# Weight sums of the second feed-forward made early, in the mixer, and kept in DRAM

## The chip, the cores and the metric

The kernel runs on one core of one Trainium2 chip. The core has five engines that run side by side, each with its own in-order list of instructions: TensorE (PE, with its weight loads shown apart as PEld), VectorE (DVE), ScalarE (ACT), GpSimd (POOL) and SyncE (SP). SP and POOL also issue the DMA transfers, which 16 DMA engines carry out. Working memory on the core is SBUF, matmul results go to PSUM, and the inputs lie in DRAM. The metric is the device time of one execution in microseconds; lower is better. The kernel before takes 2007.45 us, the median of 3 runs (2005.02 to 2007.62).

## The reference

One block of a language model on 256 tokens of width 2048, all in float32: a gated feed-forward, a mixer, a second gated feed-forward, each between two normalizations and added to its input.

```python
D_MODEL = 2048; SEQ = 256; D_FF = 5632
def _swiglu(x, w_gate, w_up, w_down):
    return (jax.nn.silu(x @ w_gate) * (x @ w_up)) @ w_down

f = _swiglu(_rmsnorm(h, ln_ffn1_pre), ffn1_gate, ffn1_up, ffn1_down)
h = h + 0.5 * _rmsnorm(f, ln_ffn1_post)
mx = _hybrid_mixer(_rmsnorm(h, ln_mix_pre), w_in, ...)   # RWKV recurrence, pooling, gates, w_out
h = h + _rmsnorm(mx, ln_mix_post)
f = _swiglu(_rmsnorm(h, ln_ffn2_pre), ffn2_gate, ffn2_up, ffn2_down)
h = h + 0.5 * _rmsnorm(f, ln_ffn2_post)
```

The mixer multiplies the tokens by a wide matrix w_in, runs a recurrence over the tokens on one part (16 heads of 64, done in 4 chunks of 64 tokens per half of the heads), sliding averages on another, and joins both through gates and w_out.

## The kernel before, in words

**Products.** The tokens are the stationary side of a matmul (128 rows of the inner dimension by 128 tokens), the weights stream through, 512 columns at a time. For accuracy each float32 operand is split into a high half (a cast to a shorter float format, on ScalarE) and a low half (operand minus high half, on VectorE), and a product is three matmuls: high by high, high by low, low by high (`mm3`, L330, lines L332 to L334). So every weight tile costs one load on SP (`get_w`, L294, into one of 4 buffers `w32`), one cast on ScalarE and one subtraction on VectorE into one of 5 buffers `wH`/`wL` (the "ring"), and then its matmuls. L308/L309 do this in the mixer, L386/L396 for pairs and L639/L644 for quads in the feed-forwards.

**Feed-forward (`ffn`, L1080).** The gate and up matrices are worked through in 11 blocks of 512 columns, two column groups at a time (f and l), then the down matrix in four groups of 512. Block 0 of the gate comes from `gemm_tok`; in the first feed-forward it goes through `head` (L794), a hand-written order for the cold start, in a list of its own. The other blocks come from `seven` (L527), which reads a string of letters. `f` and `l` are a pair: two 128-row tiles of one column group, times both token halves, 12 matmuls. `q` and `Q` are a quad: two row tiles of both column groups at once by the Strassen-Winograd scheme, 7 products instead of 8, so 21 matmuls instead of the 24 of an `f` and an `l`. For it sums of the weights are needed. With a = (f of k, l of k+1) and b = (l of k, f of k+1) they are

```python
t13 = a + (b[0], b[0])        # L622, 1024 columns
t2  = a[0] + t13[1]           # L627, 512 columns
t4  = b[1] + t2               # L631, 512 columns
```

All three are VectorE additions in a `q`. In a `Q` the first is made by a DMA instead: SP loads f of k and l of k+1 (L613), and POOL issues a transfer that adds l of k onto both (L617). In both, four casts (L639) and four subtractions (L644) follow: a (1024 columns), b (512), t13 (1024), t2 with t4 (1024). The corresponding sums of the tokens (`sums`, L435) are made once per stage and shared by the blocks.

**Order of the work.** In the feed-forwards the strings fix TensorE's order. Everything else is put in order by a planner (`Plan.solve`, L143): every operation has an engine, a duration, what it depends on, what buffers it takes, and a due time worked back from TensorE's order. It fills in the earliest operation on each engine, with the transfers' times estimated, and the result is written out as fixed lists for all five engines (`run`, L279). A load is issued at most 22 us ahead of its due time (`FETCH`). General buffers ("units") are 33 tiles of 128 x 1024 float32.

**Mixer (`mixer`).** Only TensorE's order is fixed there: generators yield pieces of matmuls, and the recurrence (`rwkv`, L1977 to L2028 for the scan over chunks) is woven with other products, so that between two of its steps stand 1.6 to 2.8 us of other matmuls, and 44 us ahead of the scan. The other engines' instructions are ordered when the program is compiled, by rank: an instruction's place in the program, or a place that is moved by `high_priority(offset=...)`; the one of lowest rank goes first among those that are ready in the compiler's own timing. The order is then fixed as a list for each engine. `tok_g` (L840) is the product of all tokens with 512 columns, and it is used for w_in and the two projections. `across` (L1047) uses it and then turns the result by a VectorE transpose and 16 small POOL transfers (L1071). The units are held by the tokens (8), the recurrence's registers (15, `R`) and what goes in and out of it. Sums and weights of the feed-forwards are not touched in the mixer.

## Time and profile before

The profile is of one execution on the chip.

| | before |
|---|---|
| median of 3 runs | 2007.45 us |
| profiled execution, its own time | 2005.37 us |
| its span, first to last instruction | 2003.7 us |
| TensorE busy | 1990.0 us, 9903 matmuls |
| VectorE busy | 1813.6 us |
| ScalarE busy | 1224.3 us |
| GpSimd busy | 410.0 us |
| moved by DMA | 472.36 MB, mean 236 GB/s |
| granted TensorE clock | 0.999 of full speed |

The first feed-forward runs from 0 to about 690 us, the mixer to about 1300, the second feed-forward to the end. How to read it: matmuls overlap each other, so the mean of one (about 390 ns) is longer than the step from one start to the next; the number of matmuls in a stretch is the better measure of TensorE's pace. Some matmul records are missing in places. A row "x <- y: total, times, longest" of the list of waits says how long the engine stood still before instruction x until y was done.

### The profile page before, as it was taken

What the parts mean: (1) busy time and instruction counts of PE and PEld (TensorE: products, weight loads), DVE (VectorE), ACT (ScalarE), POOL (GpSimd) and SP (SyncE); (2) the same over time, 40 slices, a digit from 0 to 9 for tenths busy, and PEclk for the clock granted to TensorE, in tenths of its full rate; (3) what the DMA queues carried; (4) which work ended last, traced back from release to release, by engine and by line L of the source; (5) the groups of instructions that cost most, each with busy time, mean ns of one, the idle gap of its engine ahead of it and who ended that gap; (6) DMA issues with size and microseconds to landing.
All of it is one profiled execution on the core that took longest, in us unless ns stands there. A gap on an engine that the chain in (4) does not pass through costs nothing.

```text
span 2003.7 us, 29050 instructions
## 1 busy us (share of the span) xinstructions
PE 1990.0 (99%) x9903; PEld 1644.7 (82%) x9903; DVE 1813.6 (91%) x2462; ACT 1224.3 (61%) x1631; POOL 410.0 (20%) x747
## 2 busy tenths in 40 slices
PE   9999999999999999999999999999999999999998
PEld 7888888888888888888788788888888888888886
DVE  6999999999999957799689678989999999999997
ACT  7566665676665566685466434575666656666563
POOL 2222231323000113412320111012222313230000
PEclk9999999999999999999999999999999999999999
DMA  9788798878778767757556547768888988876784
GB/s 341 226 268 270 216 304 271 254 238 257 211 229 272 264 191 210 206 174 219 147 168 189 169 158 262 263 226 276 265 269 254 276 259 244 258 242 207 232 284 158
DMA packets 253941, 472.36 MB, mean 236 GB/s; under 512 B 27363, under 2 KB 30816, under 8 KB 253792
## 3 DMA queue, kind: packets, MB, share of 16 engines
q1 hardware_dynamic: 213984, 400.89, 60.4%
q0 software_dynamic: 39520, 69.08, 15.3%
q8 instruction: 78, 1.28, 0.3%
q10 hardware_dynamic: 288, 0.52, 0.1%
q14 instruction: 71, 0.58, 0.1%
HBM read 445.45 MB, written 8.39 MB: 227 GB/s over the span
## 4 chain that ended last, share of the span: by engine, by line
PE 93%; DVE 3%; DMA 2%; issue 1%; ACT 0%; SPq 0%; DVEq 0%; POOLq 0%; POOL 0%; ACTq 0%
PE mm L332 25%; PE mm L334 24%; PE mm L333 24%; PE ms L333 5%; PE ms L334 5%; PE ms L332 5%; DMA w<-in_ffn_down_dram 1%; DVE wL L644 1%; PE tr L939 1%; DVE wL L396 1%; DMA w<-in_w_out_dram 0%; PE pA L1881 0%; DVE t L622 0%; PE mc L901 0%; DVE t L627 0%
## 5 line engine op out<-in xcount | busy, mean ns | idle before, releaser
L332 PE MATMUL mm<-wH,xH 128*128 128x512 f32 (+1 forms) x2008 | 784.3, 391 | 2.0 <-ACT wH L386 1.5
L334 PE MATMUL mm<-wH,xL 128*128 128x512 f32 (+1 forms) x2008 | 779.4, 388 | 0.1
L333 PE MATMUL mm<-wL,xH 128*128 128x512 f32 (+1 forms) x2008 | 779.3, 388 | 0.1
L332 PEld LDWEIGHTS mm<-wH,xH 128*128 128x128 f32 x2008 | 377.2, 188 | 80.9 <-ACT wH L386 1.9
L334 PEld LDWEIGHTS mm<-wH,xL 128*128 128x128 f32 x2008 | 377.0, 188 | 78.7 <-DVE xL L957 1.1
L333 PEld LDWEIGHTS mm<-wL,xH 128*128 128x128 f32 x2008 | 377.3, 188 | 75.7 <-DVE wL L309 0.4
L639 ACT CAST wH<-t 128x1024 fp32r<-128x1024 f32 x244 | 257.1, 1055 | 221.2 <-PE mm L334 121.0
L386 ACT CAST wH<-w 128x1024 fp32r<-128x1024 f32 x293 | 302.8, 1053 | 128.6 <-PE mm L334 100.8
L396 DVE TENSOR_TENSOR wL<-w,wH 128x1024 fp32r<-128x1024 f32 x293 | 351.9, 1227 | 13.8 <-ACT wH L386 12.5
L644 DVE TENSOR_TENSOR wL<-t,wH 128x1024 fp32r<-128x1024 f32 x244 | 295.7, 1234 | 10.9 <-ACT wH L639 10.2
L309 DVE TENSOR_TENSOR wL<-w,wH 128x1024 fp32r<-128x1024 f32 (+2 forms) x184 | 217.5, 1190 | 84.6 <-ACT wH L308 83.2
L308 ACT CAST wH<-w 128x1024 fp32r<-128x1024 f32 (+2 forms) x184 | 188.8, 1030 | 167.0 <-PE mm L334 147.5
L639 ACT CAST wH<-w 128x1024 fp32r<-128x1024 f32 x244 | 200.1, 837 | 109.7 <-PE mm L334 75.1
L982 POOL DMA_DIRECT2D x<-T x352 | 180.6, 608 | 389.6 <-DVE T L965 76.1
L644 DVE TENSOR_TENSOR wL<-w,wH 128x1024 fp32r<-128x1024 f32 x244 | 231.6, 966 | 0.9 <-ACT wH L639 0.9
L333 PE MATMUL ms<-wL,sH 128*128 128x512 f32 x312 | 121.5, 389 | 0.2 <-DVE wL L644 0.2
L332 PE MATMUL ms<-wH,sH 128*128 128x512 f32 x312 | 121.4, 389 | 0.0
L334 PE MATMUL ms<-wH,sL 128*128 128x512 f32 x312 | 121.4, 389 | 0.0
L617 POOL DMA_DIRECT2D t<-in_ffn_up_dram x48 | 59.8, 1256 | 230.8 <-DMA t<-in_ffn_up_dram 56.1
L631 DVE TENSOR_TENSOR t<-w,t 128x512 f32<-128x512 f32 x122 | 85.5, 701 | 0.5 <-DMA w<-in_ffn_down_dram 0.2
L627 DVE TENSOR_TENSOR t<-w,t 128x512 f32<-128x512 f32 x122 | 85.3, 700 | 0.3 <-DMA w<-in_ffn_down_dram 0.3
L622 DVE TENSOR_TENSOR t<-w,w 128x1024 f32<-128x1024 f32 x60 | 73.8, 1231 | 2.8 <-DMA w<-in_ffn_down_dram 2.8
(353 smaller groups left out, 2312.4 us busy)
## 6 DMA issues: line engine op xcount, KB each, us to landing
w<-in_w_in_dram SPq DMA_DIRECT2D x128, 512.0 KB, 4.3
w<-in_ffn_down_dram SPq DMA_DIRECT2D x104, 512.0 KB, 6.5
w<-in_ffn_up_dram SPq DMA_DIRECT2D x94, 512.0 KB, 6.0
w<-in_ffn_gate_dram SPq DMA_DIRECT2D x92, 512.0 KB, 6.6
w<-in_ffn_gate_dram SPq DMA_DIRECT2D x168, 256.0 KB, 5.5
w<-in_ffn_down_dram SPq DMA_DIRECT2D x130, 256.0 KB, 4.9
w<-in_ffn_up_dram SPq DMA_DIRECT2D x116, 256.0 KB, 5.9
t<-in_ffn_up_dram POOLq DMA_DIRECT2D x48, 512.0 KB, 8.4
```

The source lines that it names most:

```text
L308: s.nc.scalar.copy(vH, v)
L309: s.nc.vector.tensor_tensor(out=vL, in0=v, in1=vH.bitcast(F32), op=ALU.subtract)
L332: nc.tensor.matmul(ps, aH, bH, start=start, stop=False, skip_group_check=seeded)
L333: nc.tensor.matmul(ps, aH, bL, start=False, stop=False, skip_group_check=seeded)
L334: nc.tensor.matmul(ps, aL, bH, start=False, stop=stop, skip_group_check=seeded)
L386: nc.scalar.copy(x["H"], x["v"])
L396: nc.vector.tensor_tensor(out=x["L"], in0=x["v"], in1=x["H"].bitcast(F32), op=ALU.subtract)
L627: V.tensor_tensor(out=v["t24"][:, 0], in0=v["a"][:, 0], in1=v["t13"][:, 1], op=ALU.add)
L631: V.tensor_tensor(out=v["t24"][:, 1], in0=v["b"][:, 1], in1=v["t24"][:, 0], op=ALU.add)
L639: nc.scalar.copy(H, src)
L644: V.tensor_tensor(out=L, in0=src, in1=H.bitcast(F32), op=ALU.subtract)
L982: nc.gpsimd.dma_start(out=x[0][q * 32:q * 32 + 32, i], in_=src[i * 32:i * 32 + 32, q])
```

## The change

1. **Sums made ahead.** A new generator `premakes` makes, for each quad marked with the new letter `P`, the three sums t13, t2 and t4 of a weight block of the second feed-forward, and writes them to DRAM: four loads of 256 KB on SP, three additions on VectorE, two writes of 512 KB on POOL, with three units held meanwhile. `tok_g` asks for one such set after its row tiles 4, 8 and 12, in the first part of the mixer and again while and after the second half of the recurrence is woven in (`PRE_AT`), not during the first half. All of a set's instructions rank 1500 places later than where they stand (`PRE`).
2. **Second feed-forward.** It gets orders of its own (`GATE_UP2`, `DOWN2`). A `P` quad loads its sums from DRAM (two loads of 512 KB) besides three tiles of 256 KB, and makes no addition. The new orders hold 66 quads (26 q, 17 Q, 23 P), where the old hold 59 (28 q, 31 Q).
3. **First feed-forward.** It keeps 59 quads in a new order (29 q, 30 Q). The planner now takes VectorE as busy for its first 5.5 us there and ScalarE for 4.5 (`TAKEN`), and an operation that may choose a unit instead of its own kind of buffer leaves free those units that operations due earlier need (`kept_for`).
4. **Head in one list.** The list that `head` opens stays open, and the planner's order of the first feed-forward is written behind it in the same list, where before it was a second list.

```diff
-GATE_UP = ["", "fffflQlfqfllll",
-           "fqqflQQQfll", "flflQfqqQfll", ...
+    "fqfqlQQQfll", "flflqqfqQfll", ...
+GATE_UP2 = ["", "fPllfPfPqfll",
+    "flffPqPlfqll", "fqqPllqPffl", "fPfqPlPqlfl",
+    "fqfqPQflPll", "fflqQQPQfll", "fPqPllQPffl",
+    "fqfqlQQfPll", "flPPflqPqfl", "fPlqQPPlffl"]
+DOWN2 = ((0, "ffffffQfffflQqflllfqQlqlllQllQlfflll", 0),
+    (2, "fqffqQflqflQflqqqfffflQfQf", TRAIL))
+TAKEN = dict(DVE=5.5, ACT=4.5)
+PRE = 1500
+PRE_AT = ((4, 8, 12), (), (4, 8, 12))
...
+        def kept_for(n):
+            c = 0
+            for m in takers:
+                if m.due >= n.due or c > NUNITS:
+                    break
+                c += m.units
+            return c
...
-                    u, i = free[k.res[1]], HOLD if r == "ring" else SPARE
+                    u = free[k.res[1]]
+                    i = max(aside + (r == "ring"), HOLD if r == "ring" else SPARE)
...
+            def bring(i):
+                v[("t13", "t24")[i]] = s.unit((P, 2, 512), F32, ("t13", "t24")[i])
+                nc.sync.dma_start(out=v[("t13", "t24")[i]], in_=made(q)[:, i])
+            if ready_made:
+                n13, n4 = [p.op("SP", 0.4, lambda i=i: bring(i), take=[(k13, k24)[i]], size=0.52,
+                                ahead=FETCH) for i in range(2)]
...
         E = mybir.EngineType
-        with s.tc.manual_schedule(engines={E.PE, E.Activation, E.DVE, E.SP}):
+        stack = ExitStack()
+        stack.enter_context(s.listed())
+        with stack:
...
+            s.open = stack.pop_all()
...
+            if k0 in s.pre_at:
+                with s.tc.high_priority(offset=-PRE):
+                    next(s.jobs, None)
...
+    def premakes(s, wg, wu):
+        nc = s.nc
+        for b, order in enumerate(GATE_UP2):
+            quads = [c for c in order if c in "qQP"]
+            for q, c in enumerate(quads):
+                if c != "P":
+                    continue
+                k = 2 * q
+                out = s.made[b, q] = s.dp.tile([P, 2, 2, 512], F32, tag=f"made{b}_{q}",
+                                               name=f"made{b}_{q}")
+                x, y, t = [s.unit((P, 2, 512), F32, n_) for n_ in ("ma", "mb", "mt")]
+                for i in range(2):
+                    for v, w in ((x, (wg, wu)[i]), (y, (wu, wg)[i])):
+                        nc.sync.dma_start(out=v[:, i], in_=w[(k + i) * P:(k + i + 1) * P,
+                                                             b * 512:b * 512 + 512])
+                V = nc.vector
+                V.tensor_tensor(out=t, in0=x, in1=y[:, :1].to_broadcast([P, 2, 512]), op=ALU.add)
+                V.tensor_tensor(out=y[:, 0], in0=x[:, 0], in1=t[:, 1], op=ALU.add)
+                V.tensor_tensor(out=y[:, 1], in0=y[:, 1], in1=y[:, 0], op=ALU.add)
+                nc.gpsimd.dma_start(out=out[:, 0], in_=t)
+                nc.gpsimd.dma_start(out=out[:, 1], in_=y)
+                yield
+        yield True
```

More of the change, by code (lines that the diff above doesn't have):

```diff
@@ L163, in solve @@
         ready = {}
+        takers = sorted((n for n in s.nodes if any(k.res[0] == "unit" for k in n.take)),
+                        key=lambda n: n.due)
+        for n in takers:
+            n.units = sum(k.res[0] == "unit" for k in n.take)
         def add(n):
```

81 lines of the change are left out of this document (51 added, 30 removed).

## The prediction

> **What bounds the kernel now.** I read the head of the page first, then the chain of waits, the busy time by stage, and the list of what TensorE waited for.
>
> ```profile
> span 2003.7 us, 29050 instructions
> PE 1990.0 (99%) x9903; PEld 1644.7 (82%) x9903; DVE 1813.6 (91%) x2462; ACT 1224.3 (61%) x1631; POOL 410.0 (20%) x747
> PE 93%; DVE 3%; DMA 2%; issue 1%; ACT 0%; SPq 0%; DVEq 0%; POOLq 0%; POOL 0%; ACTq 0%
> ```
>
> ```profile
> 100.00:500.00 400.00, 400.00 (x1767) 331.20 (x1766) 398.59 (x481) 253.59 (x286) 107.54 (x183) 1.00 0.86 260
> 1400.00:1800.00 400.00, 400.00 (x1767) 331.31 (x1766) 397.99 (x481) 253.81 (x287) 107.58 (x183) 1.00 0.85 258
> ```
>
> ```profile
> PE mm L332 <- ACT wH L386: 1.5, 1, 1.5
> PE warm L809 <- POOL ident masks.py:199: 1.4, 1, 1.4
> PE tr L939 <- DMA x<-in_x_dram: 0.6, 2, 0.4
> PE mm L332 <- DVE u L703: 0.5, 1, 0.5
> PE pU L1977 <- DVE R L2002: 0.3, 1, 0.3
> PE ms L333 <- DVE wL L644: 0.2, 1, 0.2
> ```
>
> The columns of the stage rows are length, then busy time (count) of PE, PEld, DVE, ACT and POOL, granted clock, DMA share and GB/s. In the middle of each feed-forward TensorE starts 1767 matmuls in 400 us, one every 0.2264 us, and VectorE is busy 398.59 and 397.99 of the 400. Two engines are full at once, so I have to know which of them sets the pace. Two stretches of 25 us decide it:
>
> ```profile
> 750.00:775.00 25.00, 25.00 (x112) 20.68 (x112) 16.19 (x20) 18.61 (x33) 7.83 (x16) 1.00 0.72 211
> 1250.00:1275.00 25.00, 25.00 (x112) 20.71 (x111) 24.94 (x28) 15.25 (x17) 1.07 (x2) 1.00 0.81 299
> ```
>
> With VectorE idle a third of the time (16.19 of 25) TensorE starts 112 matmuls, with VectorE full (24.94) it also starts 112. So the pace is TensorE's own, and its listed waits add up to 4.5 us of 2003.7. The time is the number of matmuls times 0.2264 us, plus small change. A change can win by taking matmuls away, and lose by making TensorE wait where it does not wait now.
>
> A rule that reads this otherwise: the Trainium skill, Perfetto Trace Analysis, section Identifying the Most-Contended Engine, says that matmul busy time is a poor measure and that the busy share of the weight loads is the better one. That share is 82%, VectorE's in the feed-forwards 99.5%, so by the rule VectorE would be the engine to relieve. The 112 and 112 above speak against it; what it would make of the time is the third rival.
>
> **The change part by part.** The sum is made against the profiled execution: 2003.7 us of span in an execution of 2005.37 us, so 1.7 us lie around the span. The median of the runs is 2007.45, 2.1 above that execution; I carry the sum over as a difference.
>
> *1. Seven quads more in the second feed-forward.* A quad forms 7 products where two pairs form 8; a product is three matmuls (L332 to L334). Counting letters, the old orders hold 59 quads (28 q, 31 Q) and 122 pairs, the new ones for the second feed-forward 66 (26 q, 17 Q, 23 P; the title of the change says 24) and 108 pairs. TensorE loses 7 x 3 = 21 matmuls: 21 x 0.2264 = **-4.75 us**, all on the path.
>
> *2. Can VectorE follow there?* Its costs are these:
>
> ```profile
> L396 DVE TENSOR_TENSOR wL<-w,wH 128x1024 fp32r<-128x1024 f32 x293 | 351.9, 1227 | 13.8 <-ACT wH L386 12.5
> L644 DVE TENSOR_TENSOR wL<-t,wH 128x1024 fp32r<-128x1024 f32 x244 | 295.7, 1234 | 10.9 <-ACT wH L639 10.2
> L644 DVE TENSOR_TENSOR wL<-w,wH 128x1024 fp32r<-128x1024 f32 x122 | 150.3, 1232 | 0.9 <-ACT wH L639 0.9
> L631 DVE TENSOR_TENSOR t<-w,t 128x512 f32<-128x512 f32 x122 | 85.5, 701 | 0.5 <-DMA w<-in_ffn_down_dram 0.2
> L644 DVE TENSOR_TENSOR wL<-w,wH 128x512 fp32r<-128x512 f32 x122 | 85.4, 700 | 0.0
> L627 DVE TENSOR_TENSOR t<-w,t 128x512 f32<-128x512 f32 x122 | 85.3, 700 | 0.3 <-DMA w<-in_ffn_down_dram 0.3
> L622 DVE TENSOR_TENSOR t<-w,w 128x1024 f32<-128x1024 f32 x60 | 73.8, 1231 | 2.8 <-DMA w<-in_ffn_down_dram 2.8
> ```
>
> A P quad has only the four low halves: 1.232 + 0.700 + 2 x 1.234 = 4.40 us. A Q quad adds L627 and L631: 5.80. A q quad adds L622 too: 7.03. A pair costs 1.227. So VectorE changes by -2 x 7.03 - 14 x 5.80 + 23 x 4.40 - 14 x 1.227 = -11.2 us, while TensorE's time shrinks by 4.75. VectorE gets more room, 6.5 us over the stage, and the saved matmuls do not turn into a wait for it. ScalarE casts more, four per quad against one per pair, but is busy 253.81 of 400. Bytes: a q loads 1.05 MB, a Q or P 1.84, a pair 0.52; the net is +7 MB over some 600 us, 12 GB/s on 258. I cost the stage at nothing beside the -4.75. Without that cover (every net new byte waited for) 7 MB at 258 GB/s would be 27 us, but the prefetch window of 22 us in the planner makes that far from likely.
>
> *3. The sums in the mixer.* 23 times: four SP loads of 256 KB, one add of L622's kind and two of L627's (2.63 us), two POOL writes of 512 KB. In all 60.5 us of VectorE, 92 SP issues, 46 POOL issues and 23 x 2.1 = 48 MB. The stage they fall into:
>
> ```profile
> 700.00:850.00 150.00, 150.00 (x731) 127.42 (x730) 101.44 (x177) 98.82 (x171) 49.28 (x115) 1.00 0.69 202
> 850.00:1000.00 150.00, 150.00 (x1089) 121.98 (x1088) 127.29 (x240) 91.91 (x151) 38.10 (x67) 1.00 0.61 183
> 1000.00:1200.00 200.00, 199.60 (x1478) 163.05 (x1477) 155.99 (x277) 108.35 (x162) 27.90 (x44) 1.00 0.57 170
> 1200.00:1340.00 140.00, 139.46 (x644) 115.78 (x643) 124.49 (x173) 81.16 (x133) 18.35 (x35) 1.00 0.70 239
> ```
>
> VectorE is idle 500 - 384.7 = 115 us from 700 to 1200, twice the 60.5. The DMA engines are the tighter cover:
>
> ```profile
> q1 hardware_dynamic: 213984, 400.89, 60.4%
> w<-in_w_in_dram SPq DMA_DIRECT2D x128, 512.0 KB, 4.3
> w<-in_ffn_up_dram SPq DMA_DIRECT2D x94, 512.0 KB, 6.0
> L1587 POOL DMA_DIRECT2D msp<-sgb x8 | 4.5, 566 | 31.6 <-DVE R L1929 17.0 <-PE mm L334 12.4 <-DVE sgb L1586 2.1
> ```
>
> The SP queue moved 400.89 MB in 60.4% of 2003.7 us, 3.0 us per MB, so 48 MB are 146 us. From 700 to 1200 the engines are taken for 0.69 x 150 + 0.61 x 150 + 0.57 x 200 = 309 us; with 146 more it is 455 of 500, a share of 0.91. The feed-forwards run at 0.85 with no wait of TensorE, their 512 KB loads landing in 6.0 instead of 4.3 us. The weight loads have that much room:
>
> ```profile
> DVE wL L309 <- ACT wH L308: 81.3, 73, 3.0
> SPq L294 <- DVE wL L309: 262.3, 106, 7.1
> ACT wH L308 <- PE mm L334: 147.3, 93, 4.4
> ```
>
> In the mixer the split of the weights waits for TensorE to free a buffer, up to 4.4 us at a time, and the load ahead of it waits for the split: the chain runs ahead of TensorE. So 1.7 us later landing, or one add of 1.23 us ahead of a split, is hidden. The 46 POOL issues cost 46 x 0.57 = 26 us on an engine that is busy a third or less.
>
> What is not hidden is an add or a write that the compile-time order puts ahead of a step of the recurrence (L1977 to L2028), where only 1.6 to 2.8 us of other matmuls stand between steps. Behind a sum that waits for its loads on VectorE stand the state updates (L2001, L2002) and the weight splits; behind a write on POOL stand the copies of L1981 and the transposing moves of L1071; behind a load on SP, which waits for one of 33 working buffers, stand the weight loads. No row shows such a step. Bounds: nothing (low rank fills pauses only; a reshuffled order could even win a few tenths) to 60.5 us (every add exposed). I take **+1.2 us**, one 1.23-us add exposed, nearest to TensorE's present waits, of which the longest in this stage is 0.5.
>
> *4. Head in one list.* In the old order three of the next list's adds slip ahead of a weight split of the head:
>
> ```profile
> 25.68 3.49 DVE L1249 TENSOR_TENSOR nx<-xH,xL 128x1024 f32<-128x1024 f32 x3
> 29.08 1.22 DVE L309 TENSOR_TENSOR wL<-w,wH 128x1024 fp32r<-128x1024 f32 x1
> ```
>
> ```profile
> 22.82 0.60 PE L939 MATMUL tr<-ident,x 128*128 128x128 f32 x4
> ...
> 26.01 0.60 PE L939 MATMUL tr<-ident,x 128*128 128x128 f32 x4
> ...
> 29.73 0.50 PE L332 MATMUL mm<-wH,xH 128*128 128x512 f32 x1 [1.49 <-ACT wH L386]
> 30.35 0.50 PE L333 MATMUL mm<-wL,xH 128*128 128x512 f32 x1
> ```
>
> A group of the head takes 26.01 - 22.82 = 3.19 us, so the next was due at 29.20; it starts at 29.73, and its second matmul at 30.35, 0.62 later instead of 0.23. The loss is 0.53 + 0.39 = 0.9 us. (Records of that group are missing, so the 1.49 in the row overstates the gap; taken at its word with the 0.6 behind it, it bounds the gain at 2.1.) In one list the split would start at 25.68 and end before TensorE needs it: **-0.9 us**, 0 if the delayed adds are late for their own users. They feed a scaling that waits for later work anyway.
>
> *5. First feed-forward, new orders.* One Q becomes a q: VectorE +1.23 us, against 1.41 us idle in the 400 quoted above. I take 0; at worst +1.2.
>
> Sum: -4.75 - 0.9 + 1.2 = **-4.45 us**: 2000.9 on the profiled execution's scale, **2003.0** on the median's.
>
> **The rivals.**
>
> *Slower: a sum blocks the recurrence.* The sums stand in fixed places in three queues, and their loads land when the busy DMA engines let them. If one of the three adds of a sum (0.9 us on average) or the wait for its loads falls ahead of a step of the recurrence or of a buffer that its inputs need, TensorE's fixed order waits it out. Each such sum costs up to 2.63 us; two of the 23 eat nearly all of the 5.65 us of gain, from four on the kernel is slower by more than the bound. With eight, 21 - 5.65 = +15.4: 2022.8. For it: the DMA share of 0.91 and waits of POOL of tens of us behind VectorE now. Against it: the rank 1500 places later. Another cause of the same stall shows in the trace already:
>
> ```profile
> L1981 POOL COPY R<-R x8: 393/398/1224, 960.7 to 1155.8; 64x256 f32<-64x256 f32 x8
> ```
>
> The median of the eight copies is 0.40 us and one took 1.22, 0.83 more. The Trainium skill, SBUF — State Buffer, section Who interferes with whom, says that a VectorE instruction with two SBUF inputs holds the port through which GpSimd reads, and that the loser waits for its whole length; the 1224 ns fits that, and all 69 new adds have two such inputs. By that rule all 16 copies of L1981 and L1982 delayed by 0.83 us would cost 13 us; by the row, with one in eight, 2 x 0.83 = 1.7.
>
> *No change: the sums drift late.* 29050 instructions less the 9903 weight loads in 2003.7 us are 9.6 per us, so 1500 places are some 157 us (an estimate). The last seven sums, made beside the second half of the recurrence, would then rank with work that in part lies after 1200, where the row shows VectorE at 124.49 of 140 and a DMA share of 0.70. Seven sums are 18.4 us of VectorE for 15.5 us of idle time; 3 to 4 us come out as waits of TensorE, and -5.65 + 3.5 = -2.2 is left: 2005.3. Against it: the idle stretch before 1200 is long.
>
> *Faster: VectorE is the bound after all.* Then the second feed-forward shrinks by VectorE's 11.2 us instead of 4.75, and -11.2 - 0.9 + 1.2 = -10.9 gives 1996.5. Against it stand the 112 and 112.
>
> *That the change does not do what it says:* if the loads of a P quad's ready sums come late, the seven quads cost waits in the second feed-forward instead of saving; that belongs to the slower side, and the 22 us of prefetch against 6.0 us of landing make it the smaller part.
>
> **How the numbers follow.** The forecast has 0.56, the slower rival 0.24, the late drift 0.14, the VectorE bound 0.06. Differences over 0.2% (4 us) are about what a measurement of this kernel can tell from no change. The forecast's own range is 1999 to 2006 (mixer cost 0 to 3, head 0 to 2.1); at -4.45 its middle lies close to that bound, so of its 0.56 I put 0.41 on faster and 0.15 on no change. Faster: 0.41 + 0.06 = 0.47; same: 0.15 + 0.14 = 0.29; slower: 0.24. The range 1997 to 2018 leaves out half of the third rival and the worse half of the first.
>
> **What would show it.** Right: 21 fewer matmuls; the second feed-forward still at one matmul per 0.2264 us with VectorE below 99%; no gap near 29 us; TensorE waits in the mixer below 2 us together. Wrong: waits of PE for L1977 to L2028 or for weight splits of L309 between 700 and 1300; VectorE idle before the new adds with a DMA as releaser; landing times of the mixer's weight loads far over 6 us.

## The result and the profile after

The changed kernel takes **2082.07 us**, the median of 4 runs (2079.38 to 2084.57), against 2007.53 of the kernel before in the same session (4 runs, 2005.02 to 2008.81). The ratio is 1.0377 with a 95% interval of 1.0365 to 1.039: slower by 3.8%, where 0.2% faster was forecast. The head of the page of the changed kernel, its chain of waits and its DRAM traffic:

```profile
span 2077.7 us, 29453 instructions
...
PE 1998.2 (96%) x9882; PEld 1650.0 (79%) x9882; DVE 1860.5 (90%) x2513; ACT 1237.5 (60%) x1645; POOL 414.9 (20%) x778
...
HBM read 475.86 MB, written 32.51 MB: 245 GB/s over the span
...
PE 83%; DVE 6%; DMA 5%; issue 4%; ACT 1%; SPq 0%; POOL 0%; DVEq 0%; ACTq 0%; POOLq 0%
```

The 21 matmuls are gone (9903 to 9882), and yet the span is 74 us longer. The chain of waits was 93% TensorE and is now 83%: the shares of VectorE, DMA and issue grew from 3, 2 and 1% to 6, 5 and 4%. To see which stage lost, I take the matmuls that turn the input of the mixer (the first 32 of the group) and of the second feed-forward (the last 32). Rows of that group, before and after, whole and from 1200 us on; the two numbers behind the durations are the first and the last start:

```profile
L939 PE MATMUL tr<-ident,fg x64: 270/272/275, 686.8 to 1322.5; 128*128 128x128 f32 x64
L939 PE MATMUL tr<-ident,fg x32: 270/272/275, 1306.7 to 1322.5; 128*128 128x128 f32 x32
```

```profile
L1014 PE MATMUL tr<-ident,fg x64: 269/273/275, 684.6 to 1400.6; 128*128 128x128 f32 x64
L1014 PE MATMUL tr<-ident,fg x32: 269/273/275, 1384.9 to 1400.6; 128*128 128x128 f32 x32
```

The first feed-forward took 686.8 us and takes 684.6. The mixer took 1306.7 - 686.8 = 619.9 and takes 1384.9 - 684.6 = **700.3**. What comes behind it took 2003.7 - 1306.7 = 697.0 and takes 2077.7 - 1384.9 = 692.8. Both feed-forwards gained, and the mixer lost 80 us. Two stretches of the mixer, before and then after (columns as in the prediction):

```profile
760.00:860.00 100.00, 100.00 (x473) 83.95 (x472) 74.50 (x143) 67.47 (x110) 44.14 (x86) 1.00 0.73 214
860.00:960.00 100.00, 100.00 (x570) 82.52 (x570) 91.97 (x165) 64.66 (x109) 21.39 (x43) 1.00 0.66 198
```

```profile
760.00:860.00 100.00, 91.40 (x415) 74.46 (x413) 81.95 (x146) 48.58 (x69) 45.26 (x91) 0.98 1.04 356
860.00:960.00 100.00, 47.51 (x223) 39.42 (x224) 60.53 (x91) 44.07 (x85) 11.27 (x17) 0.69 0.67 229
```

From 760 to 860 the DMA engines are full, a share of 1.04 at 356 GB/s, not the 0.91 of the forecast, and TensorE starts 58 matmuls fewer. The full DMA engines alone do not explain that: from 760 to 840 they are just as full, and TensorE is still busy 78.1 of 80 us. From 860 to 960 it stands still half the time, though neither VectorE (60.53 of 100) nor the DMA engines (0.67) are full. What TensorE waited for, in the whole run:

```profile
PE pA L1960 <- DVE R L1936: 25.2, 1, 25.2
PE pV L1897 <- DVE zv L1582: 17.6, 3, 16.3
PE pn L1877 <- issue: 14.1, 1, 14.1
PE mm L366 <- ACT sga L1594: 4.7, 1, 4.7
```

Three single waits, of 14, 16 and 25 us, and all three stand at the entrance of the recurrence's first half. The longest one can be followed back, in the chain of waits of the changed kernel:

```profile
928.97 0.70 DVE mb L924
929.68 0.66 SPq L920
930.38 0.48 SPq L920
930.97 7.97 DMA mb<-in_ffn_up_dram
939.06 1.24 DVE mt L923
...
940.93 0.42 DVE zr L1582
...
954.22 0.60 DVE R L1936
954.96 4.27 PE pA L1960 x32
```

It is one sum behind another. An add of one sum ends its use of a buffer at 929.68, SP issues the loads of the next sum into it, a load lands 7.97 us later, and VectorE, which has stood at that sum's first add, makes it and only then goes on to `zr`, one of the recurrence's inputs (as are `zk` and `zv`). ScalarE, which writes the first part of `zr`, waited at the same place for a sum's write to land. Rows of VectorE and then of ScalarE, with the idle time before each in brackets:

```profile
939.06 1.23 DVE L923 TENSOR_TENSOR mt<-ma,mb 128x1024 f32<-128x1024 f32 x1 [5.60 <-DMA mb<-in_ffn_up_dram]
```

```profile
938.77 1.70 ACT L1579 ACTIVATE zr<-R,omu 128x256 f32<-128x256 f32 x4 [6.57 <-DMA made<-mb]
```

`zr` takes the working buffer that a sum's `mb` had, and may write only when `mb` has gone out to DRAM. Both waits end within 0.3 us of each other, so either of them alone would have held `zr` nearly as long. At the wait for `zv`, 45 us earlier, they can be told apart; rows of ScalarE and then of VectorE:

```profile
889.27 1.70 ACT L1579 ACTIVATE zv<-R,omu 128x256 f32<-128x256 f32 x4 [14.62 <-DMA made<-mt]
```

```profile
891.97 1.23 DVE L923 TENSOR_TENSOR mt<-ma,mb 128x1024 f32<-128x1024 f32 x1 [5.65 <-DMA ma<-in_ffn_up_dram]
893.11 0.76 DVE L1582 TENSOR_TENSOR zv<-zv,zb 128x256 f32<-128x256 f32 x2
```

ScalarE stood 14.62 us until a sum's write had left the buffer that `zv` takes. The first quarter of `zv` was then written by 889.8, but VectorE stood at the next sum's add, whose load had not landed, and came to `zv` only at 893.11, some 3.3 us later. So the larger part of this wait is the buffer that waits for a write, and the smaller one VectorE's list. The Trainium skill, TensorE: Matmul & The Clock Gate, section on the architectural detail, says that ScalarE and VectorE are strict first in, first out; these 3.3 us agree.

### The profile page after: what moved, and what is told of

Same layout as the page of the kernel before. It is cut to its first block, busy times and chain, and to the rows that moved or that the text cites. A ratio compares the mean times of both kernels' runs of the same rounds, so it can differ in the third digit from the quotient of the medians.

```text
span 2077.7 us, 29453 instructions
## 1 busy us (share of the span) xinstructions
PE 1998.2 (96%) x9882; PEld 1650.0 (79%) x9882; DVE 1860.5 (90%) x2513; ACT 1237.5 (60%) x1645; POOL 414.9 (20%) x778
## 4 chain that ended last, share of the span: by engine, by line
PE 83%; DVE 6%; DMA 5%; issue 4%; ACT 1%; SPq 0%; POOL 0%; DVEq 0%; ACTq 0%; POOLq 0%
PE mm L366 21%; PE mm L368 21%; PE mm L367 21%; PE ms L368 5%; PE ms L366 5%; PE ms L367 5%; DVE wL L343 1%; DMA w<-in_w_in_dram 1%; DMA ma<-in_ffn_up_dram 1%; DMA mb<-in_ffn_up_dram 1%; DMA R<-R 1%; PE tr L1014 1%; DMA w<-in_w_out_dram 0%; DVE pr L2006 0%; PE pA L1960 0%
## 5 line engine op out<-in xcount | busy, mean ns | idle before, releaser
L367 PE MATMUL mm<-wL,xH 128*128 128x512 f32 (+1 forms) x1966 | 766.6, 390 | 1.4 <-DVE wL L343 1.4
L368 PE MATMUL mm<-wH,xL 128*128 128x512 f32 (+1 forms) x1966 | 766.5, 390 | 0.0
L676 ACT CAST wH<-t 128x1024 fp32r<-128x1024 f32 x258 | 271.6, 1054 | 217.0 <-DVE t L668 91.2
L420 ACT CAST wH<-w 128x1024 fp32r<-128x1024 f32 x279 | 288.0, 1052 | 112.0 <-PE mm L368 89.0
L430 DVE TENSOR_TENSOR wL<-w,wH 128x1024 fp32r<-128x1024 f32 x279 | 333.8, 1219 | 17.1 <-ACT wH L420 15.5
L681 DVE TENSOR_TENSOR wL<-t,wH 128x1024 fp32r<-128x1024 f32 x258 | 310.3, 1219 | 3.5 <-ACT wH L676 1.9
L676 ACT CAST wH<-w 128x1024 fp32r<-128x1024 f32 (+1 forms) x258 | 211.3, 836 | 107.3 <-PE mm L368 81.6
L681 DVE TENSOR_TENSOR wL<-w,wH 128x1024 fp32r<-128x1024 f32 (+1 forms) x258 | 242.1, 953 | 1.2 <-ACT wH L676 1.1
L654 POOL DMA_DIRECT2D t<-in_ffn_up_dram x31 | 37.5, 1210 | 554.7 <-DMA t<-in_ffn_up_dram 257.3
L668 DVE TENSOR_TENSOR t<-w,t 128x512 f32<-128x512 f32 x106 | 72.7, 686 | 0.2
L664 DVE TENSOR_TENSOR t<-w,t 128x512 f32<-128x512 f32 x106 | 72.7, 686 | 0.0
```

The source lines that it names most:

```text
L367: nc.tensor.matmul(ps, aH, bL, start=False, stop=False, skip_group_check=seeded)
L368: nc.tensor.matmul(ps, aL, bH, start=False, stop=stop, skip_group_check=seeded)
L420: nc.scalar.copy(x["H"], x["v"])
L430: nc.vector.tensor_tensor(out=x["L"], in0=x["v"], in1=x["H"].bitcast(F32), op=ALU.subtract)
L664: V.tensor_tensor(out=v["t24"][:, 0], in0=v["a"][:, 0], in1=v["t13"][:, 1], op=ALU.add)
L668: V.tensor_tensor(out=v["t24"][:, 1], in0=v["b"][:, 1], in1=v["t24"][:, 0], op=ALU.add)
```

## The experiments

The kernels below change one thing each. "Loss" is against no_sums (2001.95 us), unless said otherwise. The kernel before, run beside each of them, gave medians from 2005.98 to 2007.34, so losses from different sessions compare to about 1.4 us.

**1. Are the sums the loss?** In no_sums no sum is made; a P quad loads plain weights in place of them.

```diff
-        s.jobs = s.premakes(ffn2_gate[0], ffn2_up[0])
-                nc.sync.dma_start(out=v[("t13", "t24")[i]], in_=made(q)[:, i])
+                c = min((cf, cl)[i], DFF - 1024)
+                nc.sync.dma_start(out=v[("t13", "t24")[i]], in_=(wf, wl)[i][k * P:(k + 1) * P, c:c + 1024] ...)
```

> The sums are not made in the mixer at all; a P quad loads two pieces of 512 KB of the weights in place of its sums, so its products are those of other numbers, while every instruction and byte of the second feed-forward stays. Both theories (working buffers: the sums hold units for which zk, zv and zr then wait; transfers: the DMA engines are full and the weight loads land late) expect the mixer back at 620 us and the rest as in the changed kernel: -2.2 in the first feed-forward, -5.4 in the second, +1.3 at the end, so 2000 to 2003 us. If it stays above 2006, part of the loss is not in the sums.

Measured: 2001.95 us (2001.38 to 2003.77), ratio 0.998 (0.997 to 0.9989). So the sums cost 80 us, and the rest of the change gains 5. The rows of no_sums for the stages:

```profile
L1016 PE MATMUL tr<-ident,fg x64: 270/272/275, 684.5 to 1323.8; 128*128 128x128 f32 x64
L1016 PE MATMUL tr<-ident,fg x32: 270/272/275, 1308.1 to 1323.8; 128*128 128x128 f32 x32
```

The mixer takes 1308.1 - 684.5 = 623.6 us here, 3.7 more than before although it holds no sum; experiment 9 comes back to that.

**2. Which sums?** late_only asks for all of them in the second half of the recurrence and behind it; own3 leaves the places alone and gives all sums the same three buffers, taken at the mixer's start.

```diff
-PRE_AT = ((4, 8, 12), (), (4, 8, 12))
+PRE_AT = ((), (), (0, 4, 8, 12))        # late_only
-                x, y, t = [s.unit((P, 2, 512), F32, n_) for n_ in ("ma", "mb", "mt")]
+                x, y, t = s.own3                # own3
```

> All 23 sums are made beside and after the second half of the recurrence (at row tiles 0, 4, 8 and 12 there), none in the first part of the mixer; everything is computed. Theory of the working buffers: zk, zv and zr of the first half come as early as before, so the 70 us of the first half go; the second half has its own z tiles and gate tiles that need units, so some 5 to 25 us are left there: 2005 to 2027. Theory of the transfers: 48 MB now fall into some 200 us instead of 400, the DMA engines are full there for longer, 2040 to 2090.

> As the changed kernel, everything computed, but all 23 sums use the same three units, taken once at the start of the mixer, so at most one sum is under way and none can take a unit from the recurrence. Theory of the working buffers (the sums under way together take all free units, and zv, zr and sga wait for their writes): zk, zv and zr come within 5 us of their old times and the loss of 80 us in the mixer falls below 10: 2000 to 2010. Theory of the transfers (48 MB fill the DMA engines wherever they fall): with one sum at a time the bursts at a share above 1.0 go too, but the weight loads still compete, 2020 to 2060. If it stays at 2070 or more, it is the place of the sums' steps in the queues.

Measured: late_only 2072.82 us, ratio 1.0331 (1.0313 to 1.0348), loss 71: the first half is as without sums, and the second half pays instead. That is far above the range that I had set for the working buffers and inside that for the transfers. own3 2161.83 us, ratio 1.0769 (1.0753 to 1.0785), loss 160, beyond the 2070 from which on I had put it down to the place of the sums' steps in the lists. Of own3, what TensorE, VectorE and ScalarE waited for longest:

```profile
PE mm L366 <- DVE yb L1791: 151.6, 3, 144.8
```

```profile
DVE mt L923 <- DMA mb<-in_ffn_up_dram: 106.2, 16, 8.2
```

```profile
ACT yb L1790 <- DVE mb L924: 140.5, 1, 140.5
```

`yb` of the pooling part was given one of the three buffers and waited 140.5 us until the last sum had left it, while VectorE made one sum after the other and stood up to 8.2 us in front of each for its loads. The list is fixed, so it could not do anything else meanwhile.

**3. The bytes alone.** copies_only moves the same number of bytes from DRAM to DRAM and makes no sum, at the sums' rank. Every byte of such a copy is both read from DRAM and written to it, so its DRAM traffic is twice that of the sums: against no_sums, copies_placed reads and writes 48 MB more each, the changed kernel 24. copies_placed makes its copies at the points of SP's list where the changed kernel starts a sum.

```diff
+                with s.tc.issue_after(s.ld.ins):     # copies_placed: behind the weight load that stands there
+                    for i in range(2):
+                        for m, w in enumerate((wg, wu)):
+                            nc.sync.dma_start(out=out[:, m, i], in_=w[(k + i) * P:(k + i + 1) * P,
+                                                                      b * 512:b * 512 + 512])
+                    for m, w in enumerate((wg, wu)):
+                        nc.sync.dma_start(out=two[:, m], in_=w[k * P:(k + 1) * P, c:c + 1024] ...)
```

> At each of the 23 places the sums' transfers stay as plain copies from DRAM to DRAM, four of 256 KB on SP and two of 512 KB on POOL, 2.1 MB as before, with the same rank; no unit is taken and VectorE adds nothing, so the P quads read weights instead of sums. Theory of the working buffers: within 6 us of the kernel without sums, 2000 to 2008. Theory of the transfers: the DMA engines are as full as before, 2050 to 2090.

> The 23 sums' bytes alone, in place: at the point of SyncE's list where the changed kernel starts a sum (after weight loads 16, 30, 33, ... 143 of the mixer's 170) it copies 4 x 256 KB and 2 x 512 KB from DRAM to DRAM, queued behind that weight load. No units, no adds, no waits on them; the ready quads of the second feed-forward read plain weights, so the output is another. Transfers (T): the burst itself makes the weight loads late; at least 50 of the 77 us that the sums cost come back, time 2050 to 2085. Units (U): without working buffers the mixer stays within 15 us of the kernel without sums, time 2002 to 2017. VectorE's list (Q): as U, 2002 to 2010.

copies_only missed its aim: 2131.27 us, ratio 1.0624, but the copies depend on nothing and were put into the first feed-forward, where they were issued from 47 to 191 us. The first feed-forward took 813.5 us, the mixer 623.6 as without them. It shows that a late rank does not hold an instruction in its place when nothing else does. copies_placed: 2028.67 us, ratio 1.011 (1.0093 to 1.0126), loss **27**. The first row is its stretch of 100 us, the second the landing of the mixer's weight loads from 700 to 1000 (count, size and median time):

```profile
760.00:860.00 100.00, 92.53 (x410) 74.67 (x409) 64.59 (x119) 57.41 (x91) 34.77 (x72) 0.98 1.01 346
```

```profile
w<-in_w_in_dram SPq DMA_DIRECT2D x78, 512.0 KB, 6.6
```

The burst is nearly as full as that of the changed kernel, and a weight load lands in 6.6 instead of the 4.3 us of the kernel before; in the changed kernel it is 5.8 in the same stretch. It costs a third of the loss; I had expected either nearly all or nearly nothing. TensorE's waits are others than in the changed kernel: 12.4 us for casts of weights and none for the entrance of the recurrence.

**4. VectorE's time alone, and with the bytes.** adds_placed puts seven small adds (2.4 us) on a tile of their own wherever VectorE's list has a sum's adds. copies_adds has these and the copies of copies_placed.

```diff
+                with s.tc.issue_after(s.sp_.ins):    # the weight split that stands there
+                    for _ in range(7):
+                        nc.vector.tensor_tensor(out=s.idle, in0=s.idle, in1=s.idle, op=ALU.add)
```

> VectorE's share of the sums alone: 23 times seven adds of 256 columns (0.34 us apart, 2.4 us for a sum's 2.5) at the places of VectorE's list where the changed kernel has a sum's adds. They read and write one small tile of their own: no loads, no writes, no units, nothing to wait for; the ready quads read plain weights, so the output is another. If VectorE's time is the price (the adds delay the recurrence that goes through VectorE): loss 20 to 45 us against the kernel without sums, time 2022 to 2047. If the price lies in waits for the loads or in units: under 10 us, 2002 to 2012.

> The DRAM copies of copies_placed (27 us of loss) and the adds of adds_placed together: the sums' bytes and the sums' VectorE time, but no units, and no add that waits for a load. If transfers and VectorE time are all, the loss comes to 65 to 85 us, time 2067 to 2087. If units, or adds that wait for their loads in VectorE's list, are a third price, it stays at the sum of the two, under 60 us: 2030 to 2060.

Measured: adds_placed 2014.92 us, ratio 1.0047 (1.0033 to 1.0061), loss **13**, between the two cases that I had set. copies_adds 2030.17, ratio 1.0122 (1.0106 to 1.0137), loss **28**. The prices do not add up. The copies make TensorE wait for weights (12.4 us for their casts in copies_placed), the adds for steps of the recurrence (the rows below); with both, only the waits for weights are left (13.9 us in copies_adds), and none of these steps waits longer than 0.3 us. With adds that wait for nothing, the sums' bytes and their VectorE time come to 28 of 80. What TensorE waited for in adds_placed:

```profile
PE pM L2025 <- DVE R L2013: 5.2, 2, 4.4
PE pA L1959 <- DVE R L1935: 3.4, 2, 2.1
```

**5. Working buffers alone.** hold3 and hold8 took 3 and 8 buffers without using them, between two one-column memsets. Nothing tied the second memset to its place, it was put right behind the first, and the buffers were free again within a microsecond.

> The kernel without sums, with three units held from the start of the mixer to the end of the first half of the recurrence: two memsets of one column each on GpSimd, no transfer and no addition (the P quads read weights instead of sums). Theory of the working buffers: zk, zv and zr wait for units, at least 30 us above the kernel without sums, 2030 to 2090. Theory of the transfers: no change against it, 2000 to 2003.

> The kernel without sums (P quads read weights instead of sums), with eight units held by memsets alone from the start of the mixer to the end of the first half of the recurrence. Theory of the working buffers: eight are more than the mixer can spare, zk, zv and zr wait, 2030 to 2090. Theory of the transfers: no change against the kernel without sums, 2000 to 2004.

They took 2001.80 and 2002.89 us and say nothing. In holdz3 and holdz6 the end is tied by data, to a copy of what is written some 150 us into the mixer.

```diff
+        s.held = [s.unit(p="hold") for _ in range(6)]            # 3 in holdz3; memset of one column each
+            if h and c0 == 0:                                    # in across: the r piece has been copied out
+                for t in s.held:
+                    nc.gpsimd.tensor_copy(t[:, 1:2], a[:, :1])
```

> The kernel without sums, with 3 working buffers taken at the mixer's start by one-column memsets on GpSimd and given back by a copy of one column of the copied-out r piece of the recurrence's input (some 150 us into the mixer), so that they are held by data until then; the output is another only because the ready quads read plain weights. No transfers, no adds. Buffers (U) and the 30 left enough at that time: zk at 130 us after the mixer's start as without sums, time 2002 (2000 to 2004).

> The same with 6 buffers, as many as two sums under way hold. U: zk finds no buffer until the 6 are given back, comes at 150 us or later in place of 130 after the mixer's start, and the first half of the recurrence starts later by it; loss 10 to 30 us, time 2012 to 2032. If buffers don't matter: zk at 130, time 2002 (2000 to 2004).

Measured: holdz3 2001.60 us, no loss. holdz6 2011.67, ratio 1.0029 (1.0018 to 1.004), loss **10**. The recurrence's input `zk` in holdz3, then in holdz6, then in the changed kernel:

```profile
L1585 ACT ACTIVATE zk<-R,omu x4: 493/494/495, 814.3 to 815.9; 128x256 f32<-128x256 f32 x4
```

```profile
L1585 ACT ACTIVATE zk<-R,omu x4: 492/494/508, 844.4 to 845.6; 128x256 f32<-128x256 f32 x4
```

```profile
L1579 ACT ACTIVATE zk<-R,omu x4: 493/494/495, 860.4 to 861.6; 128x256 f32<-128x256 f32 x4
```

Three buffers are spare, six are not: `zk` comes 30 us later with no transfer and no add in the way. The six are given back when `zk` starts, before `zv` and `zr` need theirs, so the test does not cover those two. In the changed kernel mostly two and at times three sums are under way from 770 to 940, that is six to nine buffers, each set for 17 to 35 us from its first load to the landing of its last write (by the starts of the loads and of the writes in the trace, with 6.5 us for the landing).

**6. All three without their dependences.** hold6_copies_adds is copies_adds with six buffers held as in holdz6.

> The three prices at once without their dependences: copies_adds (28 us) with holdz6's 6 buffers held through the mixer's first 150 us. No add waits for a load and no write for an add. If bytes, VectorE's time and buffers are all of it: loss 55 to 80, time 2057 to 2082. If the waits of the sums' own instructions in the lists of VectorE and GpSimd are a price of their own: under 50, time 2030 to 2050.

Measured: 2032.52 us, ratio 1.0129 (1.0112 to 1.0146), loss **31**. Bytes, VectorE's time and buffers held for 150 us come to 31 of 80 together, under the 50 that I had set for waits of the sums' own instructions as a price of their own. TensorE waits for casts of weights here too (13.7 us), and for no step of the recurrence longer than 0.7. What these kernels do not have is that the parts of a sum wait for each other: the add for its load, the write for its add, the buffer for its write.

**7. One dependence less.** no_write makes the sums and does not write them; no_add loads and writes in two buffers and does not add. In both the quads read plain weights or loaded ones.

```diff
-                nc.gpsimd.dma_start(out=out[:, 0], in_=t)      # no_write
-                nc.gpsimd.dma_start(out=out[:, 1], in_=y)
```

> The 23 sums load and add as in the changed kernel, in 3 units each, but nothing is written, and the ready quads read plain weights, so the output is another. Half of the added bytes are gone, and a sum gives its units back after its last add (about 15 us after its first load in place of 22). T: with half the bytes the share of the DMA engines stays under 1, loss under 15 of 77 us, time 2002 to 2017. U: the loss falls as the units' time does, by about a third, time about 2050 (2035 to 2065). Q (VectorE's list holds adds that wait for their loads): loads and adds are all there, loss 65 to 80, time 2067 to 2082.

> two_units without its adds: the same loads into 2 units and the same writes out of them, nothing on VectorE; the ready quads read loaded weights instead of sums, so the output is another. Transfers and units without VectorE. If units cost nothing of their own: as copies_placed, loss 20 to 35, time 2022 to 2037. If units are a price of their own: 2045 to 2075.

Measured: no_write 2049.53 us, ratio 1.0209 (1.0194 to 1.0224), loss **48**. no_add 2049.41, ratio 1.0226 (1.021 to 1.0242), loss **47**. Either cut takes off some 30 of the 80. Both times lie where I had them if the buffers that a sum holds are a price (about 2050, and 2045 to 2075). Without the writes TensorE's waits for `pn` and `pV` fall from 14.1 and 17.6 us to 0.8 and 5.0, while that for `pA` stays at 18.9 of 25.2. no_add costs 21 more than copies_placed with the same bytes; there GpSimd, which also issues the small transfers that turn the recurrence's inputs, stands in front of a sum's writes:

```profile
POOL made L923 <- DMA ma<-in_ffn_up_dram: 45.5, 10, 10.8
POOL made L924 <- DMA mb<-in_ffn_gate_dram: 42.9, 10, 9.3
```

**8. Fewer buffers, and the sums spread.** two_units makes a sum in place in two buffers. two_a is two_units with the sums asked for throughout the mixer, the first half of the recurrence included; they start from 751 to 1185 us without the pause from 930 to 1124.

```diff
-                V.tensor_tensor(out=t, in0=x, in1=y[:, :1].to_broadcast([P, 2, 512]), op=ALU.add)
-                V.tensor_tensor(out=y[:, 0], in0=x[:, 0], in1=t[:, 1], op=ALU.add)
+                V.tensor_tensor(out=x, in0=x, in1=y[:, :1].to_broadcast([P, 2, 512]), op=ALU.add)
+                V.tensor_tensor(out=y[:, 0], in0=x[:, 0], in1=y[:, 0], op=ALU.subtract)
+                V.tensor_tensor(out=y[:, 0], in0=y[:, 0], in1=x[:, 1], op=ALU.add)
+PRE_AT = ((8,), (4, 12), (4, 12))          # two_a
```

> The same sums, made in place in 2 units instead of 3 (x0+y0 and x1+y0 over x, then y0 as x0+y0-y0+x1+y0 and y1+y0 over y: one add of 0.5 us more); transfers and places as they are. U: 4 to 6 units held instead of 6 to 9, the loss falls to under a half, time 2015 to 2040. T: the bytes are the same and units free sooner let them come even closer together, loss as before or more, 2075 to 2090. Q: as before plus 23 x 0.5, 2075 to 2090.

> two_units with the sums spread: places k0=8 of the head, 4 and 12 of the first half of the recurrence and of the second, instead of 4, 8 and 12 of the head and of the second half. Five sums in the mixer's first 190 us instead of 16, some twelve in the first half, six in the second. T: no burst, share of the DMA engines under 0.95 throughout, loss under 15 us, time 2002 to 2017. U: units are shortest while the first half starts; loss like two_units or less, 2010 to 2040. Q: the sums now stand among the recurrence's own work on VectorE, a wait of up to 7 us for each of twelve: loss 50 to 90, time 2052 to 2092.

Measured: two_units 2077.40 us, ratio 1.0345 (1.033 to 1.0361), loss 75. two_a 2094.00, ratio 1.043 (1.0414 to 1.0445), loss 92. A third fewer buffers for each sum gave back 5. That is a weaker test than it looks: from 770 to 940 on average 2.3 sums were under way instead of 2.0 (counted as in experiment 5), so 4.6 buffers were taken instead of 5.9. It does not carry the theory that the number of buffers alone is the price. Spreading does not help either. The share of the DMA engines over 100 us stays at 0.95 or below, but the sums now stand among the recurrence's own work, and their waits meet it there. ScalarE in two_a:

```profile
ACT sc L1136 <- DMA made<-ma: 27.4, 1, 27.4
```

**9. Where do 3.7 us of the mixer without sums come from?** head_only has the new head and the first feed-forward's new orders, the old ones in the second, and no sums. head_alone has the old orders in both.

```diff
-        s.jobs = s.premakes(ffn2_gate[0], ffn2_up[0])
-GATE_UP2 = ["", "fPllfPfPqfll", ...              # both kernels; DOWN2 likewise
+GATE_UP2 = ["", "fffflQlfqfllll", ...
-    "fqfqlQQQfll", "flflqqfqQfll", ...           # GATE_UP and DOWN, head_alone only
+           "fqqflQQQfll", "flflQfqqQfll", ...
```

> The changed kernel with the old orders in the second feed-forward and no sums in the mixer: what is left is the head in one list and the first feed-forward's new order, all computed. Both theories: -2.5 us, from the first feed-forward, 2004 to 2005.5 where the kernel before has 2007.

> The kernel before with the head in one list, and the planner's other changes, but the old orders in both feed-forwards and no sums. The list of VectorE in the mixer ahead of the recurrence is then that of before again, where every kernel with the new orders had another one and 3.7 us more in the mixer. If that list is the cause of the 3.7: first feed-forward -2 us, mixer 619.9 as before, time 2004 to 2005.5, ratio 0.999. If it isn't (the head itself costs it): mixer 623.6, time 2007 to 2009.

Measured: head_only 2007.03 us, ratio 1.0002 (0.9992 to 1.0012). head_alone 2005.21 (2002.28 to 2007.34, 11 runs), ratio 0.9993 (0.9984 to 1.0002). Rows of head_alone:

```profile
L1014 PE MATMUL tr<-ident,fg x64: 270/272/275, 685.6 to 1321.4; 128*128 128x128 f32 x64
L1014 PE MATMUL tr<-ident,fg x32: 270/272/275, 1305.7 to 1321.4; 128*128 128x128 f32 x32
```

Its mixer takes 1305.7 - 685.6 = 620.1 us, as before. The orders of the first feed-forward shift the compiler's timing a little, and instructions of VectorE ahead of the first `pA` change places in its list (a weight split then stands before the `R L1936` that `pA` needs). In head_only TensorE waits 1.2 us for `pA`, 1.1 for `pB` and 0.6 for a gate there, and the mixer is 3.7 us longer. head_alone is the fastest of the kernels that compute everything, by 1 us, which its interval does not separate from no change.

| kernel | what it has of a sum | loss, us |
|---|---|---|
| holdz3 | 3 buffers | 0 |
| holdz6 | 6 buffers | 10 |
| adds_placed | VectorE time | 13 |
| copies_placed | bytes | 27 |
| copies_adds | bytes, VectorE time | 28 |
| hold6_copies_adds | bytes, VectorE time, 6 buffers | 31 |
| no_add | loads, writes, 2 buffers, and their waits | 47 |
| no_write | loads, adds, 3 buffers, and their waits | 48 |
| two_units | all, 2 buffers | 75 |
| the changed kernel | all, 3 buffers | 80 |

## Why the prediction was wrong, step by step

**Steps 1 and 2 were right.** The second feed-forward, from the first matmul that turns its input to its last, takes 687.1 us with the old orders (head_only) and 682.3 with the new (no_sums): -4.8 where -4.75 was forecast. The pace is unchanged, and VectorE is under 99%. Stretches of 400 us of the changed kernel in the first and the second feed-forward:

```profile
100.00:500.00 400.00, 400.00 (x1766) 331.46 (x1765) 398.97 (x481) 254.15 (x289) 113.56 (x198) 1.00 0.84 256
1480.00:1880.00 400.00, 400.00 (x1767) 331.47 (x1766) 395.70 (x467) 263.46 (x301) 92.19 (x171) 1.00 0.84 271
```

It also decides the rule that was weighed there: the time followed the count of matmuls, not VectorE's 11.2 us. The third rival is out, and so is the fear of late ready sums, since TensorE has no wait in this stage among its longer ones.

**Step 3 failed: "I take +1.2 us".** Measured are 700.3 - 623.6 = 76.7 us in the mixer, above the upper bound of 60.5, which counted the adds only. Three readings in it were wrong.
- *The DMA share of 0.91* was a mean over 500 us. The sums are not spread over them: what lets one start is that buffers are free, so fifteen started from 750 to 930, one per 12 us, and seven from 1124 to 1182, and in the first burst the share was 1.04. The room that I read from "the split waits for TensorE" did not hold 2.3 us of later landing: as copies the bytes cost 27 us. How much of the 80 they take in the changed kernel is open, since TensorE waits less than 3 us for weights there.
- *VectorE's 115 idle us* cover the adds only in part: the 2.4 us of a sum's adds cost 13 us over 23 sums. In the kernel before, VectorE was already busy 92 of the 100 us in which the recurrence starts.
- *The waits of a sum's own parts* were described and not priced. "What is not hidden is an add or a write that the compile-time order puts ahead of a step" was the right place, but the price was 2.63 us of adds where one wait is 5 to 8 us for a load and as long again for a write. By the difference to hold6_copies_adds this is the largest part, some 49 us, and 57 us of TensorE's waits (25.2, 17.6 and 14.1) stand at the entrance of the recurrence, where the trace shows the sums' own waits in front of the first two. The difference is an estimate: the prices do not add, and hold6_copies_adds gives its buffers back earlier than the sums do. That the dependences are at work is supported by cutting them (no_write and no_add, some 30 us each); how it divides between VectorE's list, GpSimd's list and buffers that wait for a write to land is not settled, because each cut changes the bytes or the buffers too.

**The slower rival was the right one**, at a chance of 0.24 and a time of 2022.8. Its mechanism, "the wait for its loads falls ahead of a step of the recurrence or of a buffer that its inputs need", is what the chain above shows. It was priced at up to 2.63 us for eight sums, the time of the adds, with no landing of a load or of a write in it; it is 76.7 / 23 = 3.3 us on average over all 23. Its counter-argument, the rank 1500 places later, did not hold the sums back: the trace has fifteen of them in a burst. My reading, which no run tests by another rank, is that rank decides among instructions that are ready in the compiler's timing, where a load is ready as soon as a buffer is; on the chip it came later, and the list could not be changed any more. The other cause named there did not show. The sixteen copies that it is about took 5.6 + 4.1 us in the kernel before and take 5.9 + 3.1 with the sums:

```profile
L2060 POOL COPY R<-R 64x256 f32<-64x256 f32 x8 | 5.9, 734 | 45.0 <-PE pS L2076 23.2 <-PE pX L2036 16.1 <-DVE R L2014 5.6
L2061 POOL COPY R<-R 64x256 f32<-64x256 f32 x8 | 3.1, 394 | 0.4
```

The late drift did not happen: the last load of the last seven sums was issued at 1184. Of the signs that the prediction named for being wrong, waits of PE and VectorE idle in front of the new adds with a DMA as releaser are there; late weight loads are the weaker one, at 5.2 us in the median of the whole run, 5.8 from 700 to 1000, and 6.6 only under the copies.

**Step 4 was too small.** -0.9 was forecast with a bound of -2.1. Matmul by matmul, head_only, no_sums and the changed kernel all gain 2.2 us against the kernel before between the 100th and the 150th matmul. Ahead of that their starts lie up to 0.4 us off, and from there to the end of the stage the difference stays the same to 0.05 us. TensorE of the changed kernel at that place:

```profile
28.80 0.39 PE L367 MATMUL mm<-wL,xH 128*128 128x512 f32 x1
29.03 0.39 PE L368 MATMUL mm<-wH,xL 128*128 128x512 f32 x1
29.26 0.39 PE L366 MATMUL mm<-wH,xH 128*128 128x512 f32 x1
```

There is no gap near 29 us, as forecast. I had set the 1.49 us of the row aside as overstated; with the 0.6 behind it, it gives the 2.1 of the bound, and that was the size.

**Step 5 was right in its stage and wrong beyond it.** The new orders cost nothing in the first feed-forward, but 3.7 us in the mixer, with instructions ahead of the first `pA` in another order. Step 3 had "a reshuffled order could even win a few tenths".

## What to carry to other kernels

A share averaged over a stage says nothing of work that starts whenever its buffers are free: here such work came in a burst, with 1.04 where the mean gave 0.91, so look at what paces it before you spread it over the idle time. Side work that loads, computes and stores costs more through its own waits in in-order lists and through buffers that wait for its stores than through its bytes and its engine time, here some 49 us against 31, as a difference of two kernels. And prices measured alone need not add, so a test with all of them and without the dependences tells more than any one of them.

## What the runs showed of the hardware

TensorE comes back slowly after a long wait. In the changed kernel the granted clock and the pace around its wait for `zv`, by stretches of 10 us and then by single matmuls:

```profile
885.00:895.00 10.00, 0.81 (x2) 0.36 (x2) 4.32 (x8) 2.98 (x8) 1.41 (x4) 0.50 0.68 214
...
905.00:915.00 10.00, 10.00 (x57) 8.66 (x56) 6.07 (x11) 6.01 (x8) 0.00 (x0) 1.00 0.51 139
```

```profile
899.54 0.63 PE L368 MATMUL mm<-wH,xL 128*128 128x512 f32 x1
899.97 0.63 PE L366 MATMUL mm<-wH,xH 128*128 128x512 f32 x1
...
901.32 0.39 PE L367 MATMUL mm<-wL,xH 128*128 128x512 f32 x1
901.55 0.39 PE L368 MATMUL mm<-wH,xL 128*128 128x512 f32 x1
```

At a granted clock of 0.50 a matmul starts every 0.43 us, and from 901 us on every 0.23 again. The Trainium skill, TensorE: Matmul & The Clock Gate, Part 1, says that TensorE's clock is halved after an idle window of about 3.4 us and let go after a busy one. The trace agrees with the halving: behind all three long waits the clock is at 0.50. The full pace is back 8.2, 7.2 and 4.7 us after the first matmul, later than one such window. Behind the two shorter waits 12 and 6 slow matmuls of 0.2 us more each cost 3.6 us; behind the longest, 32 `pA` take 4.27 us instead of the 2.34 of the kernel before. All three restarts together are little beside the waits themselves.
